# Row-wise log-sum-exp: the last four rows loaded in four unequal parts, their partial sums taken by VectorE

## The chip, the cores and the metric

The kernel runs on one core of one Trainium2 chip. The metric is the device time of one execution in microseconds (us); of several executions the median is given.

The engines that matter here are ScalarE (ACT in the profile: exponentials, logarithms, and a sum along the row if asked for), VectorE (DVE: reductions and elementwise work), TensorE (PE: two tiny matmuls), GpSimd (POOL: a few memsets) and SyncE (SP: it issues the DMA transfers).

## The reference

```python
x = np.random.randn(32, 512, 1024).astype(np.float32)
x_max = np.max(x, axis=-1, keepdims=True)
out = (x_max.squeeze(-1) + np.log(np.sum(np.exp(x - x_max), axis=-1))).astype(np.float32)
```

There are 16384 rows of 1024 float32 values, 64 MiB in all, and one float32 result for each row.

## The kernel before

The 16384 rows are spread over the 128 partitions, so each partition holds NB = 128 rows that lie next to each other in memory. "A row" below means one row in every partition: 128 x 1024 values, 512 KB.

**The fast path and its verdict.** The kernel does not look for a maximum first. It sums the plain exponentials and takes the logarithm. Then it asks whether each sum lies between LOW = 1e-18 and HIGH = 1e18. VectorE compares (`compare`, L281 to L289) with both bounds, two matmuls (L304, L307) count the answers over the partitions, a reduce (L312) makes one whole number of them, and SyncE, VectorE and ScalarE read it and branch (L316 to L321). If the count is not the expected one, a second pass with a maximum follows (L322 to L343); with this input it isn't taken.

**Chunks and the ring.** The rows come in chunks, the table `CHUNKS` at the top. An entry (r, n, p, h) means: r rows in one transfer; ScalarE takes the Exp of the first n rows in p pieces, and VectorE sums them, either by one `reduce_sum` for each piece (L255) or, with h true, "by halves", one instruction for each row that adds the row's two halves and sums the result along the way (L242). The other r - n rows ScalarE sums itself, one instruction for each row with an accumulator (L262). The chunks go through a ring of 51 rows in SBUF. SyncE issues all loads in order on one queue (`load`, L155; the last chunk at L146). Before a load it waits until the engines have finished with the rows that lie in its slots: `busy` holds, for each slot, the count of ScalarE's or VectorE's instructions to wait for. Chunks 0 to 3 fill the ring (4, 15, 16 and 16 rows); chunk 4 reuses the slots of chunks 0 and 1, and so on.

**The end.** The last four chunks have one row each. ScalarE sums them itself, into a tile `late` in PSUM; the very last one stands at L225. `take_logs` (L162) takes the logarithms in three pieces: the first 81 rows ahead of chunk 7, the next 43 rows just ahead of the last Exp, the last four after it. The first two pieces go out in one store of 124 columns (L276), the last four in one of 4 columns (L278). VectorE takes the maximum and the minimum of the 124 early sums (L293, L294), compares these two, and then, when the last Ln is done, the four late sums: K = 6 columns in all. SyncE ends when the verdict has been read and both stores have landed (L346 to L349).

**Order.** The program is written out instruction by instruction, and nothing reorders it. Each engine works through its own queue; waits are explicit counts of the semaphores `act_done`, `dve_done`, `landed` and a few more. The code of the last rows:

```python
take_logs(logged, late_row, sums[:, logged:late_row], *done_before[-LATE])
early_logs = acts
for k, (lo, hi) in enumerate(spans):
    nc.scalar.wait_ge(landed[i + k], 16)
    nc.scalar.activation(
        out=ring[:, s, lo:hi], in_=ring[:, s, lo:hi], func=Exp,
        accum_out=late[:, LATE - 1 + k : LATE + k],
    ).then_inc(act_done, 1)
```

Of the kernel before, what the change touches and what calls it, by code (L numbers as in the profile page):

```python
# [9 lines left out]
CHUNKS = [  # L10
    (4, 4, 1, False), (15, 15, 1, False), (16, 16, 2, False), (16, 16, 2, False),
    (16, 15, 2, False), (14, 14, 2, False), (13, 12, 2, False), (9, 8, 1, False),
    (7, 7, 1, True), (5, 4, 1, True), (4, 3, 1, True), (3, 3, 1, False), (2, 2, 1, True),
    (1, 0, 1, False), (1, 0, 1, False), (1, 0, 1, False), (1, 0, 1, False),
]

CUTS = ()
# [3 lines left out]
UNEVEN = ()  # L21
PARTS = ((0, 128, 2), (1, 128, 4), (3, 128, 8), (7, 64, 8), (71, 128, 8))


LN_AT = 7
LN_LAG = 1


LATE = 4
# [9 lines left out]
def kernel(  # L39
# [15 lines left out]
    assert sum(r for r, *_ in CHUNKS) == NB  # L55
# [10 lines left out]


    assert CHUNKS[-1][0] == 1
    spans = list(zip((0, *CUTS), (*CUTS, D)))
    assert 1 <= len(spans) <= 2  # L70
    n_late = LATE - 1 + len(spans)

    K = 2 + n_late

    ring = nc.alloc_sbuf_tensor("ring", [P, RING_ROWS, D], fp32).ap()
    sums = nc.alloc_sbuf_tensor("sums", [P, NB], fp32).ap()
# [3 lines left out]
    ends = nc.alloc_sbuf_tensor("ends", [P, 2], fp32).ap()  # L80
# [7 lines left out]
    TOO_MANY = 2048.0  # L88
    assert TOO_MANY > ALL_GOOD

    landed = [nc.alloc_semaphore(f"landed{i}") for i in range(len(CHUNKS) + len(spans) - 1)]
# [28 lines left out]
    for r, *_ in CHUNKS:  # L120
        if slot + r > RING_ROWS:
            slot = 0
        place.append((slot, row))
        slot += r
        row += r
# [9 lines left out]
    def load(i):  # L135
        (s, row), r = place[i], CHUNKS[i][0]
        act_wait = max(a for a, _ in busy[s : s + r])
        dve_wait = max(d for _, d in busy[s : s + r])
        if dve_wait:
            nc.sync.wait_ge(dve_done, dve_wait)  # L140
        if act_wait:
            nc.sync.wait_ge(act_done, act_wait)
        dst, src = ring[:, s : s + r], x_v[:, row : row + r]
        if i == len(CHUNKS) - 1:
            for k, (lo, hi) in enumerate(spans):
                nc.sync.dma_start(out=dst[:, :, lo:hi], in_=src[:, :, lo:hi]).then_inc(  # L146
                    landed[i + k], 16
                )
        elif i in UNEVEN:
            for first, last, step in PARTS:  # L150
                nc.sync.dma_start(
                    out=dst[first:last:step], in_=src[first:last:step]
                ).then_inc(landed[i], 16)
        else:
            nc.sync.dma_start(out=dst, in_=src).then_inc(landed[i], 16)  # L155
# [10 lines left out]

    late_row = place[-LATE][1]
    assert not any(n_dve for _, n_dve, _, _ in CHUNKS[-LATE:])

    def total(t):  # L170
        return late[:, t - late_row : t - late_row + 1] if t >= late_row else sums[:, t : t + 1]
# [38 lines left out]

    logged = 0
    done_before = [(0, 0)]
    for i, (r, n_dve, parts, by_halves) in enumerate(CHUNKS):
# [3 lines left out]
        if i == LN_AT:  # L217
            logged = place[i - LN_LAG][1]
            take_logs(0, logged, sums[:, :logged], *done_before[i - LN_LAG])
        if i == len(CHUNKS) - 1:  # L220
            take_logs(logged, late_row, sums[:, logged:late_row], *done_before[-LATE])
            early_logs = acts
            for k, (lo, hi) in enumerate(spans):
                nc.scalar.wait_ge(landed[i + k], 16)
                nc.scalar.activation(  # L225
                    out=ring[:, s, lo:hi],
                    in_=ring[:, s, lo:hi],
                    func=Exp,
                    accum_out=late[:, LATE - 1 + k : LATE + k],
                ).then_inc(act_done, 1)  # L230
                acts += 1
            continue
        nc.scalar.wait_ge(landed[i], 16 * (len(PARTS) if i in UNEVEN else 1))
        for lo, hi in cuts(n_dve, parts):
# [5 lines left out]
            if by_halves:  # L240
                for j in range(lo, hi):
                    nc.vector.tensor_tensor_reduce(  # L242
                        out=ring[:, s + j, : D // 2],
                        in0=ring[:, s + j, : D // 2],
                        in1=ring[:, s + j, D // 2 :],
                        scale=1.0,
                        scalar=0.0,
                        op0=Alu.add,
                        op1=Alu.add,
                        accum_out=sums[:, row + j : row + j + 1],  # L250
                    ).then_inc(dve_done, 1)
                    dves += 1
                    busy[s + j] = (0, dves)
            else:
# [4 lines left out]
                for j in range(lo, hi):  # L259
                    busy[s + j] = (0, dves)  # L260
        for j in range(n_dve, r):
# [8 lines left out]
        done_before.append((dves, acts))  # L270

    take_logs(late_row, NB, late[:, : NB - late_row], dves, acts)


    nc.sync.wait_ge(act_done, early_logs)
    nc.sync.dma_start(out=out_v[:, :late_row], in_=res[:, :late_row]).then_inc(stored, 16)  # L276
    nc.sync.wait_ge(act_done, acts)
    nc.sync.dma_start(out=out_v[:, late_row:], in_=res[:, late_row:]).then_inc(stored, 16)  # L278


    def compare(lo, hi, values):  # L281
        nonlocal dves
        nc.vector.tensor_tensor(  # L283
# [112 lines left out]
```

## Time and profile before

| | |
|---|---|
| time, median of 3 runs | 162.25 us (162.18 to 162.79) |
| the profiled execution's own time | 162.67 us |
| its span, first to last instruction | 161.3 us |
| VectorE busy | 121.9 us, 76% |
| ScalarE busy | 115.1 us, 71% |
| TensorE busy | 0.2 us |
| DMA queue of the loads, packets' share of the span | 97.4% |
| read from HBM | 67.11 MB |

The page's shares of busy time are means over the whole span. In this kernel all engines share one end, so the views to read are the landing times of the loads (the DMA issues give the us from issue to landing), the chain of waits, and the timeline of the last microseconds. The chain of waits puts 49% of the span on transfers into `ring`, 30% on VectorE and 20% on ScalarE.

### The profile page before, as it was taken

How to read it: one execution, taken by the hardware profiler on the slowest of the kernel's cores; microseconds unless marked ns; L12 is line 12 of the kernel's file. 1: busy time of each engine (PE TensorE's matmuls, PEld its weight loads, DVE VectorE, ACT ScalarE, POOL GpSimd, SP SyncE). 2: the span in 40 equal slices, each digit the busy share in tenths (PEclk: the TensorE clock that was granted, in tenths of full speed). 3: DMA queues.
4: the chain of work that ended last, by engine and by line, in shares of the span. 5: the costliest groups of instructions: out<-in, count | busy, mean ns of one | idle time of the engine just before them, and what ended most of it. 6: DMA issues, size and time to landing. Idle time of an engine off the chain costs nothing.

```text
span 161.3 us, 149 instructions
## 1 busy us (share of the span) xinstructions
PE 0.2 (0%) x2; PEld 0.1 (0%) x2; DVE 121.9 (76%) x51; ACT 115.1 (71%) x40; POOL 0.4 (0%) x8
## 2 busy tenths in 40 slices
PE   0000000000000000000000000000000000000000
PEld 0000000000000000000000000000000000000000
DVE  0028000003999999999999699999999999999884
ACT  3170005996079960999419993999199999999996
POOL 1000000000000000000000000000000000000000
DMA  7999799979979989989979999999999999999991
GB/s 256 508 488 442 305 472 520 439 341 520 439 341 520 423 358 520 423 358 520 423 325 455 455 455 439 423 423 423 412 402 430 436 420 410 427 436 412 417 407 42
DMA packets 2737, 67.18 MB, mean 417 GB/s; under 512 B 560, under 2 KB 560, under 8 KB 1072
## 3 DMA queue, kind: packets, MB, share of 16 engines
q1 hardware_dynamic: 2736, 67.18, 97.4%
q14 instruction: 1, 0.01, 0.0%
HBM read 67.11 MB, written 0.07 MB: 416 GB/s over the span
## 4 chain that ended last, share of the span: by engine, by line
DMA 49%; DVE 30%; ACT 20%; issue 0%; PE 0%
DMA ring<-in_x_dram 49%; DVE sums L255 29%; ACT ring L235 17%; ACT ring L262 3%; ACT ring L225 1%; ACT res L162 0%; DVE above L283 0%; PE votes L304 0%; DVE verdict L312 0%; PE votes L307 0%
## 5 line engine op out<-in xcount | busy, mean ns | idle before, releaser
L255 DVE TENSOR_REDUCE sums<-ring 128x8 f32<-128x8192 f32 (+5 forms) x14 | 111.2, 7994 | 37.3 <-ACT ring L235 37.2
L235 ACT ACTIVATE ring<-ring 128x8192 f32<-128x8192 f32 (+6 forms) x18 | 104.4, 5836 | 43.9 <-DMA ring<-in_x_dram 43.9
L242 DVE CUSTOM_DVE_ANT_0 ring<-ring 128x512 f32<-128x512 f32 x16 | 9.9, 684 | 0.0
L262 ACT ACTIVATE ring<-ring 128x1024 f32<-128x1024 f32 x8 | 8.2, 1041 | 0.0
L205 ACT ACT_TABLE_LOAD x1 | 1.3, 1283 | 0.8 <-PEq L377 0.8
L262 ACT ACTIVATION_READ_ACCUMULATOR ring<-ring 128x1 f32 x8 | 1.4, 174 | 0.0
L242 DVE DVE_READ_ACCUMULATOR2_ANT sums<- 128x1 f32 x16 | 1.3, 80 | 0.0
L225 ACT ACTIVATE ring<-ring 128x1024 f32<-128x1024 f32 x1 | 1.0, 1040 | 0.0
L283 DVE TENSOR_TENSOR above<-late,bounds 128x8 bf16<-128x8 f32 x1 | 0.2, 168 | 0.7 <-ACT res L162 0.7
L162 ACT ACTIVATE res<-sums 128x81 f32<-128x81 f32 (+1 forms) x2 | 0.5, 248 | 0.0
L312 DVE TENSOR_REDUCE verdict<-votes 1x1 int32<-1x6 f32 x1 | 0.2, 152 | 0.3 <-PE votes L307 0.3
L293 DVE TENSOR_REDUCE ends<-sums 128x1 f32<-128x124 f32 x1 | 0.3, 282 | 0.1
L304 PE MATMUL votes<-above,weights 128*1 128x6 bf16 x1 | 0.2, 167 | 160.0 <-DVE above L283 160.0
L294 DVE TENSOR_REDUCE ends<-sums 128x1 f32<-128x124 f32 x1 | 0.3, 271 | 0.0
L283 DVE TENSOR_TENSOR above<-ends,bounds 128x4 bf16<-128x4 f32 x1 | 0.2, 162 | 0.1
L162 ACT ACTIVATE res<-late 128x4 f32<-128x4 f32 x1 | 0.2, 173 | 0.0
L304 PEld LDWEIGHTS votes<-above,weights 128*1 128x1 bf16 x1 | 0.1, 80 | 160.0 <-DVE above L283 160.0
L307 PE MATMUL votes<-above,weights 128*1 128x6 bf16 x1 | 0.2, 165 | 0.0
L225 ACT ACTIVATION_READ_ACCUMULATOR ring<-ring 128x1 f32 x1 | 0.2, 153 | 0.0
L206 POOL MEMSET bounds<- 128x6 f32 x1 | 0.1, 104 | 0.4 <-POOLq L377 0.4
L207 POOL MEMSET bounds<- 128x6 f32 x1 | 0.1, 104 | 0.0
L377 POOL MEMSET const-bfloat16-1.0<- 128x1 bf16 x1 | 0.1, 103 | 0.0
(6 smaller groups left out, 0.6 us busy)
## 6 DMA issues: line engine op xcount, KB each, us to landing
ring<-in_x_dram SPq DMA_DIRECT2D x1, 7680.0 KB, 25.1
ring<-in_x_dram SPq DMA_DIRECT2D x1, 7168.0 KB, 28.6
ring<-in_x_dram SPq DMA_DIRECT2D x1, 6656.0 KB, 35.7
ring<-in_x_dram SPq DMA_DIRECT2D x1, 4608.0 KB, 20.3
ring<-in_x_dram SPq DMA_DIRECT2D x2, 2048.0 KB, 16.2
ring<-in_x_dram SPq DMA_DIRECT2D x1, 3584.0 KB, 28.5
ring<-in_x_dram SPq DMA_DIRECT2D x1, 2560.0 KB, 27.5
ring<-in_x_dram SPq DMA_DIRECT2D x4, 512.0 KB, 27.2
```

What stands on the lines that cost most here:

```text
L162: nc.scalar.activation(out=res[:, lo:hi], in_=src, func=Ln, bias=bias).then_inc(act_done, 1)
L205: nc.scalar.preload_act_table_set("natural_log_exp_and_others")
L225: nc.scalar.activation(out=ring[:, s, lo:hi], in_=ring[:, s, lo:hi], func=Exp, accum_out=late[:, LATE - 1 + k : LATE + k],).then_inc(act_d ...
L235: nc.scalar.activation(out=ring[:, s + lo : s + hi], in_=ring[:, s + lo : s + hi], func=Exp).then_inc(act_done, 1)
L242: nc.vector.tensor_tensor_reduce(out=ring[:, s + j, : D // 2], in0=ring[:, s + j, : D // 2], in1=ring[:, s + j, D // 2 :], scale=1.0, scal ...
L255: nc.vector.reduce_sum(out=sums[:, row + lo : row + hi], in_=ring[:, s + lo : s + hi], axis=AX).then_inc(dve_done, 1)
L262: nc.scalar.activation(out=ring[:, s + j], in_=ring[:, s + j], func=Exp, accum_out=total(row + j),).then_inc(act_done, 1)
L283: nc.vector.tensor_tensor(out=above[:, :, lo:hi], in0=values.unsqueeze(1).to_broadcast([P, 2, hi - lo]), in1=bounds[:, :, lo:hi], op=Alu.i ...
L293: nc.vector.reduce_max(out=ends[:, :1], in_=sums[:, :late_row], axis=AX).then_inc(dve_done, 1)
L294: nc.vector.tensor_reduce(out=ends[:, 1:], in_=sums[:, :late_row], axis=AX, op=Alu.min).then_inc(dve_done, 1)
L304: nc.tensor.matmul(votes[:1, :K], lhsT=weights[:, :1], rhs=above[:, 0], start=True, stop=False)
L307: nc.tensor.matmul(votes[:1, :K], lhsT=weights[:, 1:], rhs=above[:, 1], start=False, stop=True).then_inc(counted, 1)
```

## The change

There are two parts. The first is a new table of chunks: how many rows of each chunk VectorE sums, in how many pieces and in which way. The second is the end of the input: the last four rows are no longer four transfers of one row, but one flat stretch of 4096 values in each partition, cut at 1536, 2688 and 3456 into parts of 1.5, 1.125, 0.75 and 0.625 rows. ScalarE takes the Exp of each part as it lands. VectorE sums the first three parts by halves: the piece of each row that a part holds is one instruction, and where a row is continued the instruction starts from the row's sum so far. The last part ScalarE sums itself into `late`, and the last Ln gets VectorE's partial sum of that row as its bias.

With this, the Ln pieces are now the first 67 rows (ahead of chunk 6), the next 60 after the last Exp, and the last row. The first store (67 columns) is issued right after the last loads, the second (61 columns) after the last Ln. The maximum and minimum are taken over the first 94 sums, between the two reduces of chunk 7; the compare takes these two and the other sums one by one, K = 37 columns. The first load, the ring and the second pass are as before.

```diff
 CHUNKS = [
-    (4, 4, 1, False), (15, 15, 1, False), (16, 16, 2, False), (16, 16, 2, False),
-    (16, 15, 2, False), (14, 14, 2, False), (13, 12, 2, False), (9, 8, 1, False),
-    (7, 7, 1, True), (5, 4, 1, True), (4, 3, 1, True), (3, 3, 1, False), (2, 2, 1, True),
-    (1, 0, 1, False), (1, 0, 1, False), (1, 0, 1, False), (1, 0, 1, False),
+    (4, 0, 1, False), (15, 15, 1, False), (16, 16, 1, False), (16, 14, 2, False),
+    (16, 13, 2, False), (14, 12, 2, False), (13, 11, 2, False), (9, 8, 2, False),
+    (7, 6, 1, False), (5, 4, 1, True), (4, 3, 1, True), (3, 3, 1, True), (2, 2, 1, True),
 ]
-CUTS = ()
+LAST_ROWS = 4
+CUTS = (1536, 2688, 3456)
-LN_AT = 7
-LN_LAG = 1
-LATE = 4
+LOG_AT, LOG_UPTO = 6, 4
+EARLY = 6
...
-    K = 2 + n_late
+    K = NB - early_rows + 2 + 1
...
+    def halves(s, row, lo=0, hi=D):
+        nonlocal dves
+        half = (hi - lo) // 2
+        nc.vector.tensor_tensor_reduce(
+            out=ring[:, s, lo : lo + half],
+            in0=ring[:, s, lo : lo + half],
+            in1=ring[:, s, lo + half : hi],
+            scale=1.0,
+            scalar=total(row) if lo else 0.0,
+            op0=Alu.add,
+            op1=Alu.add,
+            accum_out=total(row),
+        ).then_inc(dve_done, 1)
+        dves += 1
+        parts_done[row] = dves
...
+    nc.scalar.wait_ge(pool_done, 1)
...
+                if i == EARLY + 1 and not lo:
+                    nc.vector.wait_ge(dve_done, done_after[EARLY][0])
+                    for k, op in enumerate((Alu.max, Alu.min)):
+                        nc.vector.tensor_reduce(
+                            out=all_sums[:, NB + k : NB + k + 1],
+                            in_=sums[:, :early_rows],
+                            axis=AX,
+                            op=op,
+                        ).then_inc(dve_done, 1)
+                        dves += 1
...
+    s, row = place[-1]
+    wait_free(s, LAST_ROWS)
+    here, there = flat(ring[:, s : s + LAST_ROWS]), flat(x_v[:, row:])
+    for k, (lo, hi) in enumerate(spans):
+        nc.sync.dma_start(out=here[:, lo:hi], in_=there[:, lo:hi]).then_inc(
+            landed[len(CHUNKS) + k], 16
+        )
+
+    nc.sync.wait_ge(act_done, logs_done)
+    nc.sync.dma_start(out=out_v[:, :logged], in_=res[:, :logged]).then_inc(stored, 16)
+    for k, (lo, hi) in enumerate(spans):
+        last = k == len(spans) - 1
+        nc.scalar.wait_ge(landed[len(CHUNKS) + k], 16)
+        nc.scalar.activation(
+            out=here[:, lo:hi],
+            in_=here[:, lo:hi],
+            func=Exp,
+            accum_out=late[:, :1] if last else None,
+        ).then_inc(act_done, 1)
+        acts += 1
+        if not last:
+            rows = list(range(lo // D, -(-hi // D)))
+            if lo % D:
+                rows = rows[1:] + rows[:1]
+                nc.vector.wait_ge(dve_done, parts_done[row + lo // D])
+            nc.vector.wait_ge(act_done, acts)
+            for j in rows:
+                halves(s + j, row + j, max(lo - j * D, 0), min(hi - j * D, D))
+    summed = acts
+    take_logs(logged, NB - 1, sums[:, logged : NB - 1], dves, done_after[-1][1])
+    take_logs(NB - 1, NB, late[:, :1], parts_done[NB - 1], summed, bias=total(NB - 1))
     nc.sync.wait_ge(act_done, acts)
-    nc.sync.dma_start(out=out_v[:, late_row:], in_=res[:, late_row:]).then_inc(stored, 16)
+    nc.sync.dma_start(out=out_v[:, logged:], in_=res[:, logged:]).then_inc(stored, 16)
...
-    nc.vector.wait_ge(act_done, done_before[-LATE][1])
+    nc.vector.wait_ge(act_done, done_after[-1][1])
     nc.vector.wait_ge(dve_done, dves)
-    nc.vector.reduce_max(out=ends[:, :1], in_=sums[:, :late_row], axis=AX).then_inc(dve_done, 1)
-    nc.vector.tensor_reduce(
-        out=ends[:, 1:], in_=sums[:, :late_row], axis=AX, op=Alu.min
-    ).then_inc(dve_done, 1)
-    dves += 2
-    nc.vector.wait_ge(pool_done, 1)
-    nc.vector.wait_ge(dve_done, dves)
-    compare(0, 2, ends)
+    compare(above[:, :, : K - 1], all_sums[:, early_rows:])
     nc.vector.wait_ge(act_done, acts)
-    compare(2, K, late[:, :n_late])
+    compare(above[:, :, K - 1 :], late[:, :1])
```

## The prediction

> **What bounds the kernel now.** I read the page's DMA parts first, then the landing times by issue, then the timeline of the last 12 us.
>
> The page, DMA queues:
>
> ```profile
> q1 hardware_dynamic: 2736, 67.18, 97.4%
> ...
> HBM read 67.11 MB, written 0.07 MB: 416 GB/s over the span
> ```
>
> The timeline of SyncE, and the DMA issues of the same moment (size, us from issue to landing):
>
> ```profile
> 130.07 0.47 SPq L146 DMA_DIRECT2D ring<-in_x_dram  x1
> ```
>
> ```profile
> ring<-in_x_dram SPq DMA_DIRECT2D x1, 512.0 KB, 28.3
> ```
>
> The queue's packets fill 97.4% of the span, and the last load, issued at 130.07, lands 28.3 us later, at 158.4. Read one by one in the same way, the single rows land at 154.6 (128.74 + 25.9), 157.2 (129.59 + 27.6) and 158.4: 1.27 us for each 512 KB. So the loads stream without a hole, and nothing on an engine can move 158.4 unless it lets the queue run dry.
>
> The timeline after that:
>
> ```profile
> 157.35 1.05 ACT L262 ACTIVATE ring<-ring 128x1024 f32<-128x1024 f32 x1
> 157.56 0.69 DVE L242 CUSTOM_DVE_ANT_0 ring<-ring 128x512 f32<-128x512 f32 x1
> 158.17 0.08 DVE L242 DVE_READ_ACCUMULATOR2_ANT sums<- 128x1 f32 x1
> 158.30 0.16 ACT L262 ACTIVATION_READ_ACCUMULATOR ring<-ring 128x1 f32 x1
> 158.35 0.24 ACT L162 ACTIVATE res<-sums 128x43 f32<-128x43 f32 x1
> ...
> 158.49 1.04 ACT L225 ACTIVATE ring<-ring 128x1024 f32<-128x1024 f32 x1
> 158.56 0.27 DVE L294 TENSOR_REDUCE ends<-sums 128x1 f32<-128x124 f32 x1
> 158.61 0.35 SPq L276 DMA_DIRECT2D out_dram<-res  x1
> 158.94 0.16 DVE L283 TENSOR_TENSOR above<-ends,bounds 128x4 bf16<-128x4 f32 x1
> 159.44 0.15 ACT L225 ACTIVATION_READ_ACCUMULATOR ring<-ring 128x1 f32 x1
> 159.62 0.17 ACT L162 ACTIVATE res<-late 128x4 f32<-128x4 f32 x1
> 159.82 0.34 SPq L278 DMA_DIRECT2D out_dram<-res  x1
> ```
>
> The end is a short chain: landing 158.4, Exp of one row 158.49, Ln 159.62 to 159.79, store issued 159.82. The span ends at 161.29. Two things run to that end side by side: the last store (landing 1.4 us after its issue, 161.23), and the verdict (compare, matmuls, reduce, branch), after which SyncE has cleared its semaphores at 161.21 by the trace's sequencer records. Only these 2.9 us behind 158.4 can be shortened.
>
> **The change, part by part.** *The new distribution of rows* (CHUNKS): rows on VectorE's sums go from 119 to 107, rows that ScalarE sums itself, up to chunk 12, from 5 to 17. The groups by form (busy, mean ns of one):
>
> ```profile
> L255 DVE TENSOR_REDUCE sums<-ring 128x6 f32<-128x6144 f32 x2 | 13.0, 6544 | 0.0
> L235 ACT ACTIVATE ring<-ring 128x3072 f32<-128x3072 f32 x2 | 5.5, 2756 | 0.2 <-DMA ring<-in_x_dram 0.2
> L235 ACT ACTIVATE ring<-ring 128x2048 f32<-128x2048 f32 x1 | 1.9, 1892 | 0.0
> ```
>
> The DMA issues, the two stores:
>
> ```profile
> out_dram<-res SPq DMA_DIRECT2D x1, 62.0 KB, 2.2
> ...
> out_dram<-res SPq DMA_DIRECT2D x1, 2.0 KB, 1.4
> ```
>
> A reduce of r rows takes 1.067r + 0.15 us (3.35 for 3, 6.54 for 6, 8.68 for 8), and the next begins 0.08 before its end; a half-sum of a row begins every 0.613 (timeline of 143.9 to 152.5). An Exp of r rows takes 0.853r + 0.19, and the next begins 0.09 before its end; an Exp that sums a row, about 1.05. Chunk 0's four rows, now summed by ScalarE, take it from 7.54 to 11.8; it then idles until 25.88, so they cost 0, as does its new wait for GpSimd's memsets, which end at 1.0.
>
> Does this starve the loads? They wait for slots. Chunk 2 becomes one Exp and one reduce: Exp 45.23 to 59.1, reduce to 76.3; this frees chunk 5's load (72.28 before). Chunk 3's two reduces of 7 end at 83.9 and 91.4; chunk 6's load waits for the second: 91.4 instead of 80.87. Its bytes are wanted when chunk 5's have gone, shortly before 100.85, so 8 us or more are left. Chunks 7 and 8 issue at 105.5 (107.2 before), chunk 9 at 112.7, the last four rows at 128.4 (128.74). So the stream is unchanged: cost 0. If that cover were gone, each us without work would be a us of time. The first store, now 67 columns, is issued at about 130 behind the last loads in the same queue, and cannot delay them.
>
> *The last loads*: 768, 576, 384 and 320 KB at 1.27 us per 512 KB: from chunk 12's landing at 153.35 to 155.26, 156.69, 157.64, 158.43. The same bytes, the same end.
>
> *ScalarE at the end*: chunk 12's Exp starts at 153.57 as now and leaves ScalarE free at 155.36. The parts take 1.47, 1.15, 0.83 and 0.72 (0.853r + 0.19; no form below one row is in the trace: between 0.72 and the 1.04 of a whole row for the last, which would add up to 0.32; I take the straight line, which all forms from 1 to 15 rows follow). They start at 155.36, 156.74, 157.80 and 158.53. The last one's accumulator is read by 159.31, against 159.59 now: **-0.28**. The Ln over the early rows (43 columns, 0.14 from its start to the next, 158.35 to 158.49) has moved from ahead of the last Exp to behind it. It may start 0.05 after the read has started (158.30 to 158.35 now), at 159.21, and the last Ln 0.14 later, 159.35; the read ends at 159.31, so this costs **+0.01**. Its own cover is that read. But it now waits for all of VectorE's half-sums.
>
> *VectorE at the end* is busy without a break from 121.9: chunk 6 to 133.8, chunk 7 with the minimum and maximum moved between its reduces (0.2 each, now beside the loads) to 142.8, chunk 8 one reduce of 6 to 149.3, chunk 9 four half-sums to 151.7, chunk 10 to 153.6. Chunk 11 waits for its Exp: 153.68 to 155.5, chunk 12 to 156.75. The first part's Exp ends at 156.83: row 0 from 156.85 to 157.46, then 256 columns of row 1. For short half-sums the trace has only the 512-column row: 0.613. Bounds: nothing of it scales (0.613 each), or all but the 0.08 of the accumulator read does. I take the second: reduces show 1.04 ns per column, which makes 0.533 of the 0.613. Then 256 columns cost 0.35, 320 0.41, 192 0.28. A wait of VectorE for itself shows at L294 to L283: end 158.83, next start 158.94, so 0.11 after the end. Part two therefore starts not at 157.9 but at 157.97, and ends at 158.73; part three, whose Exp ends at 158.63, starts at 158.77 and hands over its last sum at **159.43** (start of its last piece, 159.06, + 0.28 + 0.09, as 158.26 follows 157.56 now). The 60-column Ln starts at 159.45 instead of 159.21, **+0.24**, and the last Ln at 159.59, against 159.62. A start value or a bias read through a pointer is in no row; I take 0 for each of the three, ends 0 and 0.11, the price of the other small wait just shown; nothing in them can gain.
>
> The Trainium skill, "VectorE: DVE Perf Modes" (The DRAIN you can't avoid), says that a semaphore between chained operations costs nothing extra; the rows above show 0.11 behind an operation's end with a wait, and a start 0.08 before its end without one (L293, 158.36 and 0.28 long, to L294, 158.56). By the rule the end would be about 0.1 earlier; the trace decides.
>
> *The last store* has 61 columns (30.5 KB) instead of 4 (2 KB). Rows: 1.4 us for 2 KB, 2.2 for 62 KB; so +0 to +0.8. Of the 62 KB store's sixteen completions fifteen came 1.40 to 1.55 us after the issue and one at 2.24, while one packet of the instruction queue ran 0.61 us from 159.51; the 2 KB store's came at 1.25 to 1.41. I take halfway between 1.41 and 1.55: **+0.07**. [...]
>
> *The verdict* counts 37 columns instead of 6: the wide compare ends by 159.75, ahead of the last Ln; the two matmuls and the reduce over 31 more columns at 1.04 ns add 0.03 to 0.05, so the verdict ends at 161.23, under the store.
>
> Sum against the profiled execution (span 161.29, its own time 162.67): -0.28 + 0.01 + 0.24 + 0.07 = **+0.04**, so 162.71 there. The median of the runs shown, 162.25, lies 0.42 below that execution; the forecast is 162.25 + 0.04, rounded **162.3**.
>
> **The rivals.** *VectorE is in time.* If the short pieces or the self-wait cost a little less, the 60-column Ln starts at 159.21 and the last Ln at 159.35: -0.27 + 0.07, **162.05**. For it: ScalarE is only 0.2 ahead. Against: VectorE has no pause between 121.9 and 153.6, and enters the parts late.
>
> *VectorE becomes the bound* (the other side). If a short half-sum costs the 0.613 of a full one, part one ends at 158.07, part two at 159.49, and the last sum is handed over at 160.80: the last Ln starts 1.34 later than now, **163.66** with the store. Five short pieces are in the chain; from 0.15 us more for each it decides, since 5 x 0.154 + 0.04 = 0.81. For it: no short form is in the trace. Against: the reduces are straight lines.
>
> *The last store meets a straggler* as the first did at 159.51: -0.03 + 0.83, **163.05**. For it: the store has become more like the first one. Against: one instruction packet in the span, and it may fall elsewhere.
>
> *The stream runs dry* because chunk 6's load is issued 10.5 us later: **163.3** for each us missing beyond the 8. Only a far slower 16-row reduce would do it.
>
> **How the numbers follow.** Forecast 0.62, VectorE in time 0.18, VectorE the bound 0.08, straggler 0.08, dry stream 0.04. 162.3 is the likeliest. The range goes from below the second case, 161.9, to just under the straggler, 163.0; about 2 in 10 is outside. 0.5% is 0.81 us, about what a measurement of this kernel can tell from no change: 161.44 and 163.06. The first two cases and half the straggler are within; slower is most of the bound, half the straggler and the dry stream, 0.11; a gain of 0.81 would have to come from the 2.9 us behind the last landing, 0.03.
>
> **What would show it.** Last load landing at 158.4 to 158.5; last Exp starting near 158.53, 0.72 long; half-sums of 256, 320 and 192 columns starting 0.35, 0.41 and 0.28 apart; the last of them ending near 159.4 and the 60-column Ln waiting for VectorE; the store landing in 1.45 to 1.5. It is wrong if the last landing moves, if a short half-sum takes 0.6, or if the store takes 2.

## The result and the profile after

| | before | after |
|---|---|---|
| time, median of 6 runs each | 162.5 us (162.18 to 162.92) | 163.34 us (163.19 to 163.56) |
| ratio of the times | | 1.0051, 95% interval 1.0032 to 1.0071 |
| the profiled execution's own time / span | 162.67 / 161.29 | 163.19 / 161.81 |
| last load lands (of the 16 DMA engines that carry it, the last one's completion) | 158.42 | 157.95 |
| from there to the end of the span | 2.87 | 3.86 |

The kernel is 0.84 us slower, 0.5%, and the whole interval lies above 1; the forecast of a tie was wrong, and 163.34 lies above the range. Of the 1.05 us between the forecast (162.29 before it was rounded) and 163.34, 0.25 is the level (before measures 162.5 here, 162.25 in the three runs that the forecast started from); 0.80 is the change (0.84 instead of 0.04). The part of the time that lies outside the span is 1.37 us in both kernels, so all of it lies in the span. One profile's landing says little: in e4, e9, e12 and e16 below, which issue the same loads, it lies at 158.41, 158.08, 158.27 and 158.68, and in this profile it came 0.47 earlier than in that of before. What can be compared is the stretch behind it, which is 0.99 longer.

The page's DMA queues of the kernel after (packets, MB, share of 16 engines' span), and two of its DMA issues (KB, us from issue to landing):

```profile
q1 hardware_dynamic: 2736, 67.18, 96.8%
q14 instruction: 2, 0.02, 0.0%
```

```profile
ring<-in_x_dram SPq DMA_DIRECT2D x1, 320.0 KB, 28.4
...
out_dram<-res SPq DMA_DIRECT2D x1, 30.5 KB, 1.5
```

The loads stream as before, and the last store takes what was forecast. The second line is the clue: two packets of the instruction queue where the kernel before has one (both of 8192 bytes; their times, here and below, are those of the trace's DMA records). The timeline of the last microseconds of the kernel after (start, us, engine, line, operation; in brackets idle time ahead of it and who ended it):

```profile
157.61 0.49 DVE L204 CUSTOM_DVE_ANT_0 ring<-ring 128x320 f32<-128x320 f32 x1
...
158.03 0.48 DVE L204 CUSTOM_DVE_ANT_0 ring<-ring,sums 128x256 f32<-128x256 f32 x1
158.44 0.08 DVE L204 DVE_READ_ACCUMULATOR2_ANT sums<- 128x1 f32 x1
158.73 0.15 ACT L294 ACTIVATION_READ_ACCUMULATOR ring<-ring 128x1 f32 x1
158.75 0.36 DVE L204 CUSTOM_DVE_ANT_0 ring<-ring 128x192 f32<-128x192 f32 x1 [0.23 <-DVE sums L204]
...
159.03 0.41 DVE L204 CUSTOM_DVE_ANT_0 ring<-ring,sums 128x192 f32<-128x192 f32 x1
159.37 0.08 DVE L204 DVE_READ_ACCUMULATOR2_ANT sums<- 128x1 f32 x1
159.56 0.24 DVE L221 TENSOR_TENSOR above<-sums,bounds 128x72 bf16<-128x72 f32 x1
159.86 0.25 ACT L150 ACTIVATE res<-sums 128x60 f32<-128x60 f32 x1 [0.98 <-DVE above L221]
160.02 0.24 ACT L150 ACTIVATE res<-late,sums 128x1 f32<-128x1 f32 x1
160.28 0.34 SPq L316 DMA_DIRECT2D out_dram<-res  x1
```

Two holes are to be seen. First, VectorE's piece of 192 columns starts at 158.75, 0.72 behind the start of the piece ahead of it (158.03); a piece of 256 columns with a start value is elsewhere followed after 0.41 (e6, e16). Its Exp had ended by 158.2, and the engine stands idle for 0.23. Second, the 60-column Ln starts at 159.86. VectorE's last sum was handed over at 159.47 by the trace's semaphore records, and VectorE's own wide compare, which waits for the same sum, starts at 159.56. A sequencer is the part of an engine that goes through the program in order, stands at its waits and hands the work on; the waits and branches in the trace are its records. By the records of ScalarE's sequencer the wait had gone through at 159.49, so 0.37 pass between the wait and the Ln; elsewhere such a step takes 0.06 (e5, 159.78 to 159.84). The waits name the compare as the releaser:

```profile
ACT res L150 <- DVE above L221: 1.0, 1, 1.0
```

That is the last event ahead of the Ln, not its cause, as the fourth experiment shows. Each hole is worth 0.31 us (0.72 less 0.41, 0.37 less 0.06).

### The profile page after: what moved, and what is told of

The parts are those of the page before. It is cut to its first block, busy times and chain, and to the rows that moved or that the text cites. A ratio compares the mean times of both kernels' runs of the same rounds, so it can differ in the third digit from the quotient of the medians.

```text
span 161.8 us, 175 instructions
## 1 busy us (share of the span) xinstructions
PE 0.2 (0%) x2; PEld 0.1 (0%) x2; DVE 113.5 (70%) x54; ACT 117.0 (72%) x60; POOL 0.5 (0%) x8
## 3 DMA queue, kind: packets, MB, share of 16 engines
q1 hardware_dynamic: 2736, 67.18, 96.8%
## 4 chain that ended last, share of the span: by engine, by line
DMA 43%; ACT 34%; DVE 22%; issue 1%; SPq 0%; PE 0%; DVEq 0%
DMA ring<-in_x_dram 43%; ACT ring L243 29%; DVE sums L253 20%; ACT ring L271 4%; DVE ring L204 1%; ACT ring L294 1%; DVE above L221 0%; SPq L140 0%; ACT res L150 0%; PE votes L324 0%; DVE verdict L332 0%; DVE sums L204 0%; PE votes L327 0%; DVEq L319 0%; DVEq L307 0%
## 5 line engine op out<-in xcount | busy, mean ns | idle before, releaser
L253 DVE TENSOR_REDUCE sums<-ring 128x6 f32<-128x6144 f32 (+5 forms) x13 | 102.6, 7941 | 46.2 <-ACT ring L243 46.2
L243 ACT ACTIVATE ring<-ring 128x6144 f32<-128x6144 f32 (+7 forms) x17 | 94.0, 5564 | 36.1 <-DMA ring<-in_x_dram 36.1
L271 ACT ACTIVATE ring<-ring 128x1024 f32<-128x1024 f32 x17 | 17.7, 1041 | 5.4 <-DMA ring<-in_x_dram 5.4
L204 DVE CUSTOM_DVE_ANT_0 ring<-ring 128x512 f32<-128x512 f32 (+3 forms) x16 | 9.4, 637 | 0.4 <-DVE sums L204 0.2
L294 ACT ACTIVATE ring<-ring 128x1536 f32<-128x1536 f32 (+3 forms) x4 | 3.9, 1042 | 0.0
L271 ACT ACTIVATION_READ_ACCUMULATOR ring<-ring 128x1 f32 x17 | 3.2, 187 | 0.0
L150 ACT ACTIVATE res<-sums 128x67 f32<-128x67 f32 (+1 forms) x2 | 0.5, 248 | 1.0 <-DVE above L221 1.0
L204 DVE CUSTOM_DVE_ANT_0 ring<-ring,sums 128x256 f32<-128x256 f32 (+1 forms) x2 | 0.9, 448 | 0.0
L294 ACT ACTIVATION_READ_ACCUMULATOR ring<-ring 128x1 f32 x1 | 0.2, 151 | 0.0
```

Source lines behind the costliest of these rows:

```text
L150: nc.scalar.activation(out=res[:, lo:hi], in_=src, func=Ln, bias=bias).then_inc(act_done, 1)
L204: nc.vector.tensor_tensor_reduce(out=ring[:, s, lo : lo + half], in0=ring[:, s, lo : lo + half], in1=ring[:, s, lo + half : hi], scale=1.0 ...
L243: nc.scalar.activation(out=ring[:, s + lo : s + hi], in_=ring[:, s + lo : s + hi], func=Exp).then_inc(act_done, 1)
L253: nc.vector.reduce_sum(out=sums[:, row + lo : row + hi], in_=ring[:, s + lo : s + hi], axis=AX).then_inc(dve_done, 1)
L271: nc.scalar.activation(out=ring[:, s + j], in_=ring[:, s + j], func=Exp, accum_out=total(row + j),).then_inc(act_done, 1)
L294: nc.scalar.activation(out=here[:, lo:hi], in_=here[:, lo:hi], func=Exp, accum_out=late[:, :1] if last else None,).then_inc(act_done, 1)
```

## The experiments

In a recorded text, a letter stands for the theory told beside it; F is the instruction fetch below. The times of all runs first; "span" and "outside" (time less span) are medians over the runs of a kernel, "behind" is the stretch from the last landing to the end in its profiled execution. The runs of before beside them gave 162.44 to 162.6 us, span 161.1 to 161.2, outside 1.36 to 1.38. The median span less "behind" is an estimate of where the last load lands in a median run: 158.3 for the kernel before and 158.1 for the kernel after.

| kernel | us | ratio, interval | span | outside | behind |
|---|---|---|---|---|---|
| e1 new table, old end | 162.92 | 1.0021 [1.0013, 1.0030] | 161.3 | 1.62 | 3.1 |
| e2 old table, new end | 164.29 | 1.0094 [1.0078, 1.0109] | 162.9 | 1.35 | 4.5 |
| e3 no carried sum | 163.16 | 1.0035 [1.0022, 1.0047] | 161.75 | 1.41 | 3.3 |
| e4 compare last | 163.83 | 1.0074 [1.0061, 1.0088] | 162.45 | 1.38 | 4.1 |
| e5 ScalarE shifted | 163.15 | 1.0046 [1.0031, 1.0061] | 161.8 | 1.36 | 3.5 |
| e6 VectorE shifted | 163.52 | 1.0061 [1.0048, 1.0074] | 162.2 | 1.35 | 3.5 |
| e7 both shifted | 163.18 | 1.0043 [1.0031, 1.0055] | 161.85 | 1.34 | 3.2 |
| e8 e7, cut at rows | 163.07 | 1.0037 [1.0024, 1.0050] | 161.7 | 1.37 | 2.9 |
| e9 no fetch in the span | 163.33 | 1.0065 [1.0050, 1.0079] | 161.45 | 1.90 | 3.2 |
| e10 e9, cut at rows | 163.11 | 1.0044 [1.0031, 1.0057] | 161.2 | 1.90 | 2.9 |
| e11 before, longer program | 162.63 | 1.0011 [1.0002, 1.0019] | 161.3 | 1.35 | 2.9 |
| e12 VectorE's fetch hidden | 163.25 | 1.0038 [1.0024, 1.0051] | 161.6 | 1.72 | 3.4 |
| e13 fetch hidden, cut at rows | 163.20 | 1.0043 [1.0029, 1.0057] | 161.8 | 1.37 | 3.5 |
| e14 e1, fetches hidden | 162.70 | 1.0014 [1.0003, 1.0024] | 161.3 | 1.36 | 3.1 |
| e15 both placed, cut at rows | 162.57 | 1.0009 [0.9999, 1.0019] | 161.2 | 1.37 | 3.0 |
| e16 both placed, own cuts | 162.97 | 1.0026 [1.0017, 1.0036] | 161.6 | 1.34 | 3.4 |

**First round: which part of the change, and is it the small waits?** e1 has the new table of rows and keeps the old end; e2 has the new end with the old table.

```diff
 CHUNKS = [
-    (4, 0, 1, False), (15, 15, 1, False), (16, 16, 1, False), ...
+    (4, 4, 1, False), (15, 15, 1, False), (16, 16, 2, False), ...
```

The first edit is e2's, against the kernel after; e1 keeps the upper table, with the four single rows and the code of the kernel before.

> The new distribution of rows with the four single rows of before at the end (their sums by ScalarE, 43-or-more-column Ln ahead of the last Exp, 4-column store). Theory A (the loss is all in the new end, where two Ln wait for VectorE's partial sums): as the kernel before, ratio 0.998 to 1.002, about 162.2 to 162.7 us; the last landing to the last Ln's start is 1.2 us as before. Rival B (the new distribution costs time): 163.2 to 163.5.

> The old distribution of rows up to chunk 12 with the new four parts at the end. Theory A: the loss is here, and larger, since chunk 11 goes back to one reduce of 3.35 us and VectorE enters the parts about 1.4 us later than in the changed kernel: 164.2 to 164.8. Rival B (the distribution costs it): 162.2 to 162.7.

e1 loses 0.37 of the 0.84, but only 0.1 of it in the span (161.3 against 161.2); the rest is outside, 1.62 instead of 1.37. That was a riddle until the third round. e2 is much slower. Its timeline:

```profile
154.23 3.35 DVE L253 TENSOR_REDUCE sums<-ring 128x3 f32<-128x3072 f32 x1 [1.36 <-ACT ring L243]
...
161.42 0.25 ACT L150 ACTIVATE res<-sums 128x60 f32<-128x60 f32 x1 [1.57 <-DVE sums L204]
```

With the old table VectorE still reduces chunk 11 until 157.6 and hands over its last sum at 161.33. So the new end needs the new table; neither is good alone. One more thing is to be seen in e2: its ScalarE program is shorter (45 records instead of 68), and its Ln stands 0.06 behind its wait. The hole is gone there.

e3 lets each carried piece start at zero and writes it to a spare column, so that VectorE waits for itself once less in parts two and three; the earlier part of such a row is left out of the sum. e4 moves the wide compare behind the last Ln, which also puts it on the path of the verdict.

```diff
-            scalar=total(row) if lo else 0.0,
+            scalar=0.0,
...
-            accum_out=total(row),
+            accum_out=spare(row) if lo else total(row),
...
-                nc.vector.wait_ge(dve_done, parts_done[row + lo // D])
```

> The changed kernel in which a continued row's piece goes to a spare column from 0.0, without the pointer to the sum so far and without VectorE's wait for itself; the second pieces of rows 125 and 126 are left out of the results. Theory A with the carry as its price (the 0.11 and 0.22 us waits behind VectorE's own semaphore, and pointer pieces 0.065 longer): the last piece is handed over at 159.0 instead of 159.47, and the time falls by 0.4 to 0.5 us. If the 60-column Ln then starts at once behind the accumulator's read, 0.8. Rival C (the carry costs nothing, only the number of pieces counts): 0.1 at most.

```diff
+    nc.vector.wait_ge(act_done, acts)
     compare(above[:, :, : K - 1], all_sums[:, early_rows:])
-    nc.vector.wait_ge(act_done, acts)
     compare(above[:, :, K - 1 :], late[:, :1])
```

> The changed kernel with VectorE's wide compare behind the last Ln instead of beside the 60-column Ln. In the changed kernel that Ln starts 0.37 us after its semaphore, 0.05 after the compare's end. Rival D (the compare, reading the same sums, holds the Ln up): the Ln starts within 0.1 of its semaphore, at 159.55, and the store 0.3 us earlier, while the verdict gets 0.25 longer; time 0.0 to 0.2 below the changed kernel's. Theory E (the compare has nothing to do with it): the gap stays 0.37 and the time rises by 0.2 to 0.25.

e3 gains about 0.2 of the 0.84, half of what was expected: the carried pieces' 0.065 each and the hole at the third part are gone (VectorE's packet now runs at 157.65, and no hole goes with it), the hole ahead of the Ln stays (0.37). e4 shows that the releaser named by the waits is innocent:

```profile
159.83 0.08 DVE L204 DVE_READ_ACCUMULATOR2_ANT sums<- 128x1 f32 x1
160.31 0.25 ACT L150 ACTIVATE res<-sums 128x60 f32<-128x60 f32 x1 [0.98 <-DVE sums L204]
...
160.85 0.24 DVE L221 TENSOR_TENSOR above<-sums,bounds 128x72 bf16<-128x72 f32 x1 [0.93 <-ACT res L150]
```

VectorE has nothing but its sums ahead of the Ln now, and the Ln still starts 0.48 behind the start of the last read, as in the kernel after (159.37 to 159.86). So the compare is not the cause. The time rose by some 0.4 us, twice what was expected.

**The theory that remained.** In each trace with a hole, an 8 KB packet of the instruction queue follows 1.0 to 1.15 us behind the start of the wait at which the sequencer stood, and that place is the same in the engine's program: ScalarE's at the 62nd to 64th record of the trace, VectorE's at the 51st to 53rd, with a dozen instructions of the second pass ahead of it in its program. So the theory is: at about its 64th instruction a sequencer stops for some 0.3 us, and the next block of the program is fetched. If its engine has work queued, nobody sees it. If the stop falls behind a wait that has just ended, it is paid in full. The engine does not wait for the packet's bytes: the Ln starts at 159.86, the packet at 160.51. What the sequencer does in the 0.3 us, and that the packet brings the next block, no record shows; what can be tested is that the stop belongs to a place of the program. The kernel before has one packet in its span (159.51); by the same count VectorE's stop there lies beside the reduces at L293 and L294, and ScalarE's program with 47 records never gets that far. The Trainium skill, "Runtime: NRT & Kernel Launch" (Instruction fetch mechanics), has the sequencer fetch blocks of 256 instructions in the same way and calls the crossing mostly hidden; here the packets have 8192 bytes, and the crossing is hidden or costs 0.31, by where it falls. The measurement decides.

**Second round: shift the stop.** e5 puts eight one-column Exps at the start of ScalarE's program, e6 eight one-column memsets at the start of VectorE's, e7 both, and e8 cuts the last rows at 1024, 2048, 3072 and 3456 as well, so that no row but the last is carried on.

```diff
-CUTS = (1536, 2688, 3456)
+CUTS = (1024, 2048, 3072, 3456)
...
+    for k in range(8):
+        nc.vector.memset(dummy_v[:, k : k + 1], 0.0)
...
+    for k in range(8):
+        nc.scalar.activation(out=dummy[:, k : k + 1], in_=bounds[:, 0, :1], func=Exp)
```

> The changed kernel with eight tiny Exp (one column each, into a tile nobody reads) at ScalarE's start, where it waits for the first load anyway; nothing else differs, so ScalarE's later instructions stand eight places further on in its program. Theory F (at a fixed place of its program an engine's sequencer stops for 0.3 to 0.4 us to have the next block of instructions fetched; it shows where the instruction there stands right behind a wait that has just ended): the 60-column Ln starts 0.06 us after its semaphore wait instead of 0.37, and the time falls by 0.3. Rival G (the 0.37 belongs to that Ln itself, behind an idle ScalarE): the gap stays 0.37 and the time is unchanged within 0.1.

> The changed kernel with eight one-column memsets at VectorE's start, where it is idle for 38 us, so that VectorE's later instructions stand eight places further on. Theory F: the first piece of part three starts 0.41 us after the piece before it instead of 0.72, and the time falls by 0.3. Rival G (the gap is the price of a continued piece and of the wait for its sum): it stays 0.72, the time is unchanged within 0.1.

> Both shifts together. Theory F: both gaps go, the time falls by 0.5 to 0.65 from the changed kernel's, to a ratio of 1.001 to 1.002 to the kernel before; what is left is VectorE's lateness, as the prediction had it. Rival G: unchanged, ratio 1.005.

> Both shifts, and the last four rows cut at 1024, 2048, 3072 and 3456: three whole rows, then 384 and 640 columns of the last. No row but the last is continued, so there is no carry and no wait of VectorE for itself; ScalarE has one Exp more. Theory F with VectorE's lateness as the rest of the loss: VectorE hands over its last sum before the last accumulator is read, the 60-column Ln starts right behind that read, ratio 0.997 to 1.000. Rival H (the rest of the loss is the store and the verdict of 37 columns, or ScalarE's own lateness): ratio 1.001 to 1.003.

Each hole goes with its own engine's shift and only with it. e5, the last read of VectorE and the Ln behind it:

```profile
159.66 0.08 DVE L205 DVE_READ_ACCUMULATOR2_ANT sums<- 128x1 f32 x1
159.84 0.25 ACT L151 ACTIVATE res<-sums 128x60 f32<-128x60 f32 x1 [0.67 <-DVE sums L205]
```

e6, the second piece of part two, the first of part three, and the Ln:

```profile
159.00 0.48 DVE L205 CUSTOM_DVE_ANT_0 ring<-ring,sums 128x256 f32<-128x256 f32 x1
...
159.41 0.35 DVE L205 CUSTOM_DVE_ANT_0 ring<-ring 128x192 f32<-128x192 f32 x1
...
160.51 0.25 ACT L151 ACTIVATE res<-sums 128x60 f32<-128x60 f32 x1 [0.66 <-DVE above L222]
```

In e5 the Ln follows the read's start by 0.18 instead of 0.48, while the hole at part three stays. In e6 part three follows after 0.41, and the Ln keeps its 0.48. In e7 both are gone, and in e8 the stretch behind the last landing is 2.88, that of before. So both holes belong to places in the programs. The time does not follow: by the ratios e5, e7 and e8 win back only 0.08, 0.13 and 0.23 us, where 0.3 and more was expected, and e6 loses another 0.16. The packets had moved into the stream of loads (ScalarE's to 121.0 to 121.1, VectorE's to 153.9 to 154.1; where no wait held it up, ScalarE's sequencer was far ahead of its engine, which starts its 62nd record only at 150.7 in e5). There a packet takes 0.31 to 0.33 us. Each load is spread over 16 DMA engines, and it has landed when the slowest has. In e7 the sixteen completions of chunk 12, ahead of VectorE's packet, lie within 0.87 us; of those of the first part, behind it, fifteen lie within 0.86 us (154.32 to 155.18), and the last comes 0.71 later, at 155.89. One engine stays behind like this to the end, and the last landing is at 159.07. By the estimate above the last load lands at 158.7 to 158.8 in e6, e7 and e8, some 0.4 later than in the kernel before, but at 158.3 in e5, which has only the early packet among its loads.

**Third round: no fetch in the span, and the fetch alone.** e9 shortens VectorE's program by moving the second pass's code behind it and ScalarE's by giving chunk 0 back to VectorE; e10 is e9 with cuts at rows. e11 is the kernel *before* with forty one-column Exps ahead, which only puts a fetch into its stream.

```diff
-    (4, 0, 1, False), (15, 15, 1, False), ...
+    (4, 4, 1, False), (15, 15, 1, False), ...
...
-    with nc.body("second_vector", valid_engines=vector):
...
+    with nc.body("second_vector", valid_engines=vector):
```

```diff
+    nc.scalar.wait_ge(pool_done, 1)
+    for k in range(40):
+        nc.scalar.activation(out=idle_a[:, k : k + 1], in_=bounds[:, 0, :1], func=Exp)
```

> The changed kernel with both engines' programs shortened instead of lengthened: VectorE's code of the second pass stands behind the first pass and not ahead of it, and chunk 0's four rows are one Exp and one reduce again, seven instructions fewer on ScalarE. No place of the 64th instruction is reached before the verdict, so no block of instructions is fetched in the span. Theory F with its second half (the fetched 8 KB, where it falls among the loads, holds one of the sixteen DMA engines up and delays the last landing; that is why shifting forward did not pay in time): from the last landing to the end 3.2 us instead of 3.86, the last landing as in the changed kernel, ratio 1.000 to 1.002. Rival I (shifting bought nothing in time because something else then ends last): ratio 1.004 to 1.005 as in the changed kernel.

> The same, with the last four rows cut at 1024, 2048, 3072 and 3456, so that no row but the last is continued. Theory F: 2.9 us from the last landing to the end, as in the kernel before and in the shifted kernel with these cuts, and no fetch among the loads: ratio 0.997 to 1.000, the only version here that could beat both. Rival I: 1.003 to 1.004, as with the forward shift.

> The kernel before with forty one-column Exp at ScalarE's start, where it waits for loads until 25.9 us, so that ScalarE's 64th instruction falls at about 130 to 136 us, among the loads and while ScalarE has work queued. Theory F, second half: one 8 KB instruction packet among the loads, no gap on an engine, and the last landing 0.3 to 0.5 us later: ratio 1.002 to 1.003. Rival J (8 KB more on one of sixteen engines is nothing beside 4 MB): ratio 0.999 to 1.001.

The stretch behind the last landing becomes what was expected: 3.23 in e9, 0.63 less than in the kernel after, which is the two holes, and 2.94 in e10. The spans fall, e10's to within 0.1 of that of before, and the time stays, against both theories: the packets run behind the last instruction (e9: 162.04 and 162.37), and the time outside the span grows from 1.37 to 1.90 us. That was e1's riddle too: its packet stands at 163.12. e11 costs 0.18 us (interval 0.03 to 0.31), between what the two theories expected, so it does not decide between them. Its packet ran at 126.5, and behind it, too, one DMA engine lags (the completions of chunk 6 lie within 0.65 us; of chunk 7 fifteen lie within 0.65, and one comes at 1.14), but in its profile the last load lands at 158.40, no later than in that of before.

**Fourth round: hide them.** e12 (chunk 0 back to VectorE, three memsets) puts VectorE's stop behind part two's first piece; e13 shortens ScalarE's program further (chunks 3 and 4 in one Exp) and cuts at rows; e14 is e1 with eight memsets, so that ScalarE's stop falls beside a running Exp and VectorE's at the first compare, which has time to spare.

```diff
-    (4, 0, 1, False), (15, 15, 1, False), ...
+    (4, 4, 1, False), (15, 15, 1, False), ...
...
+    for k in range(3):
+        nc.vector.memset(idle_v[:, k : k + 1], 0.0)
```

```diff
-    (4, 0, 1, False), (15, 15, 1, False), (16, 16, 1, False), (16, 14, 2, False),
-    (16, 13, 2, False), ...
+    (4, 4, 1, False), (15, 15, 1, False), (16, 16, 1, False), (16, 14, 1, False),
+    (16, 13, 1, False), ...
...
-CUTS = (1536, 2688, 3456)
+CUTS = (1024, 2048, 3072, 3456)
```

> The changed kernel with chunk 0's four rows as one Exp and one reduce (ScalarE's program seven instructions shorter, so it has no fetch) and three one-column memsets at VectorE's start: its stop then falls behind the first piece of part two, while that piece runs and after the loads' packets. Theory F with a price for every place: no gap at part three and none at the 60-column Ln, 3.2 us from the last landing to the end, 1.38 to 1.39 outside the span, ratio 1.001 to 1.003. Rival K (the time outside the span grows whenever the gaps go): ratio 1.004 to 1.005 again.

> The same aim with the cuts at 1024, 2048, 3072 and 3456; chunk 3 and 4 have one Exp and one reduce each in place of two, so that VectorE's stop falls behind the compare of the four last columns, where it waits for the verdict's matmuls anyway. Theory F: 2.9 from the last landing to the end, 1.38 outside the span, ratio 0.998 to 1.001. Rival K: 1.003 to 1.004.

> The new distribution with the old end, whose VectorE program was too short to reach its 64th instruction in the span (its profiled execution had 1.56 us outside the span), with eight one-column memsets at VectorE's start, so that the stop falls at the first compare, which has 2 us to spare. Theory F: 1.38 outside the span, ratio 1.000 to 1.001 instead of 1.0021. Rival B (the distribution itself costs 0.3 us): 1.002.

Neither e12 nor e13 reaches the ratio that was expected; both come out near rival K. e12 has no hole at part three or at the Ln, but 0.11 of VectorE's stop shows (the piece of 320 columns is followed after 0.53 instead of 0.42), and a packet runs behind the end (162.38, 1.03 behind ScalarE's branch), outside 1.72. In e13 a packet falls on the last store, at 160.36 for 0.56 us:

```profile
out_dram<-res SPq DMA_DIRECT2D x1, 30.5 KB, 2.1
```

The store takes 2.1 us instead of 1.5 and ends the kernel, while the verdict was through at 161.0. This is the straggler of the prediction, at 0.6 us instead of the 0.8 priced there. So e13's time does not show rival K: outside the span it has 1.37. e14 is the cleanest reading of the table: outside the span 1.36, and **the new distribution of rows alone costs 0.1 us by the medians, 0.23 by the ratio** (interval 0.05 to 0.39), with whatever of the two stops still shows. That lies between the expectation and rival B's 0.3, which the interval does not exclude.

**Fifth round: both where they cost nothing.** Was the loss explained in full? e15 and e16 place each stop behind the landing of one of the last parts, beside work, ahead of the last store: three one-column Exps, three or four memsets, and a wait that is fulfilled already (so that the one behind it becomes an instruction of the sequencer alone); e15 has one more wait on VectorE, and the cuts at rows. The edit of e16:

```diff
+    for k in range(4):
+        nc.vector.memset(idle_v[:, k : k + 1], 0.0)
...
+    for k in range(3):
+        nc.scalar.activation(out=idle_a[:, k : k + 1], in_=bounds[:, 0, :1], func=Exp)
...
+        if k == 2:
+            nc.scalar.wait_ge(act_done, 1)
         nc.scalar.wait_ge(landed[len(CHUNKS) + k], 16)
```

> The changed kernel with cuts at 1024, 2048, 3072 and 3456, and the instruction packets of both engines placed on purpose: three one-column Exps and three one-column memsets ahead of the programs, and two waits split off, so that each sequencer reaches its stop behind the landing of one of the last parts, while its engine still has work. Fetch theory: no idle time in the middle of the end, both packets between 158 and 159.3, so neither among the loads nor on the last store; end 2.9 us behind the last landing, 1.37 us outside the span, span about 161.2, ratio 0.999 to 1.001. If the loss has another part (the table, the parts as such), the span stays above 161.5 and the ratio is 1.002 or more with all of these signs in place.

> The changed kernel with its own cuts, and both instruction packets placed in the same way (three one-column Exps, four memsets, one wait split off ahead of the Exp of the third part). Fetch theory: the first piece of the third part 0.41 us behind the piece before it, the 60-column Ln 0.06 us behind its wait, packets between 158.4 and 159.2, end 3.2 us behind the last landing, 1.37 us outside the span, span about 161.45, ratio 1.001 to 1.002: the predicted tie, less the time that VectorE is late. If the packets are not the cause, the ratio stays at 1.004 or more.

e15, the packets and the end (packets at 158.45 and 159.34):

```profile
q14 instruction: 3, 0.02, 0.0%
```

```profile
158.72 0.36 DVE L206 CUSTOM_DVE_ANT_0 ring<-ring 128x192 f32<-128x192 f32 x1
...
159.01 0.15 ACT L302 ACTIVATION_READ_ACCUMULATOR ring<-ring 128x1 f32 x1
159.19 0.25 ACT L152 ACTIVATE res<-sums 128x60 f32<-128x60 f32 x1
...
159.34 0.24 ACT L152 ACTIVATE res<-late,sums 128x1 f32<-128x1 f32 x1
159.61 0.34 SPq L326 DMA_DIRECT2D out_dram<-res  x1
```

(The third packet is one of 24 bytes at the start.) The Ln starts 0.03 behind the end of ScalarE's own read (159.16); VectorE's last sum, whose wait ends at 159.12, is in time. Span 161.2, outside 1.37, ratio 1.0009: a tie, as expected. So with cuts at rows the new table, the flat stretch in parts and the wider store and compare together cost about 0.1 us (interval 0 to 0.3) once the stops and packets are out of the way. e16, with the change's own cuts:

```profile
158.36 0.49 DVE L206 CUSTOM_DVE_ANT_0 ring<-ring 128x320 f32<-128x320 f32 x1
...
158.90 0.48 DVE L206 CUSTOM_DVE_ANT_0 ring<-ring,sums 128x256 f32<-128x256 f32 x1
...
159.31 0.35 DVE L206 CUSTOM_DVE_ANT_0 ring<-ring 128x192 f32<-128x192 f32 x1
...
160.10 0.25 ACT L152 ACTIVATE res<-sums 128x60 f32<-128x60 f32 x1 [0.47 <-DVE sums L206]
```

No hole at part three or at the Ln, packets at 158.95 and 159.49; 1.0026 where 1.001 to 1.002 was expected. Part of VectorE's stop still shows: the 256-column piece starts 0.53 behind the 320-column one instead of 0.42. Without those 0.11 the Ln would start 1.31 us behind the last landing (158.68), still 0.29 later than the forecast's 1.02. No version here beats the kernel before.

## Why the prediction was wrong

- *The stream is unchanged:* right; 96.8% of the span in packets, the last part 28.4 us from issue to landing, and by the estimate above the last landing is no later than in the kernel before (158.1 and 158.3).
- *ScalarE's parts:* right; the last Exp is 0.72 long, as the straight line had it. It starts 0.15 behind the landing in the kernel after.
- *Short half-sums scale:* right; behind pieces of 256, 320 and 192 columns the next starts after 0.35 (e3), 0.42 and 0.28, so the rival in which VectorE becomes the bound by 0.613 for each is out. The wait for itself costs 0.12, where 0.11 was taken from the rows of before. None of the other rivals took place in the kernel after either.
- *The last store, +0.07:* right, 1.46 us.
- *The failed step: "The 60-column Ln starts at 159.45 instead of 159.21, +0.24".* It started at 159.86, and the last landing came 0.48 earlier than in the forecast, so it is 0.89 late, counted from the landing (1.91 instead of 1.02). That VectorE's last sum came at 159.47, where 159.43 was forecast, is a coincidence of that early landing. The 0.89 are: 0.31, VectorE's sequencer stop ahead of part three; 0.31, ScalarE's ahead of the Ln; and about 0.27 of small terms. Of these, 0.06 is the step from a semaphore to ScalarE's instruction (0.08 without the stop, taken as 0.02), 0.06 the start value read through a pointer (taken as 0; a piece with one takes 0.48 instead of 0.42), 0.10 the first part's Exp, which starts 0.20 behind its landing instead of 0.10, 0.05 and 0.03 the starts of parts two and three; -0.04 and 0.01 make up the rest. The two stops were in no step and no rival: the forecast put 0.02 between the hand-over of VectorE's last sum and the Ln, and 0.39 passed (159.47 to 159.86).
- *The last Ln with its bias from a pointer, taken as 0, ends 0 and 0.11:* it takes 0.24 instead of 0.17 us, +0.07, inside its bounds. With the 0.89, the store's 0.04 and some 0.03 of steps, less the 0.04 that the forecast gains from the landing to the last Ln, it makes up the 0.99.
- *The prediction saw the instruction packet* and used it for the store only: "one instruction packet in the span, and it may fall elsewhere". It did not ask whose packet it was. The count of instructions answers that, by the reading above: ScalarE's program grows from 47 records to 68, past the place where VectorE's already stopped.

The share of each cause in the median is not settled to a tenth: most kernels without a fetch in the holes pay for it in the stream, on the store or outside the span. That e15 ties and e16 loses 0.48 us bounds it: with the stops hidden, the change's own cuts cost some 0.3 to 0.4 us more than cuts at rows (where only the last row is carried on), and the stops about the same again (0.84 less 0.48). The median spans of e9 and e10, with no packet in them, say the same: 0.35 and 0.1 above before, where the kernel after has 0.8 to 0.9. That the time outside the span grows by 0.3 to 0.5 us when a packet runs there was seen in e1, e9, e10 and e12, but nothing here shows what waits for it.

## What to carry to other kernels

Where an end of a few tenths decides, count the instructions of each engine's program, not only their durations: find the packets of the instruction queue in the trace, see at which instruction each engine's sequencer stops, and whether the change moves such a stop behind a wait. Here a stop was best placed beside queued work, behind the last load and ahead of the last store (e15). And compare the stretch from the last landing to the end, not the absolute times of two profiles: the landing itself lay 0.7 us apart here in kernels that issue the same loads. Then check by the runs' times that the stretch's gain has not gone somewhere else, as it did in e7, e9 and e13.

## What the runs showed of the hardware

- At one place of its program, counted here as about the 64th instruction, a sequencer stops for 0.3 us, and 1.0 to 1.15 us behind the wait at which that shows a packet of 8192 bytes runs for 0.31 to 0.70 us. Beside work no cost could be told (e15, a tie), behind a wait a stop costs 0.31. A packet on a last store cost 0.6 (e13, 2.1 instead of 1.5 us).
- A load's landing is that of the slowest of 16 DMA engines: the last load's completions lie 0.5 us apart in the kernel after, 0.7 in that of before, and 1.0 in e16, also without a packet among the loads. Behind a packet one of the sixteen falls back, by 0.71 us in e7 and 0.49 in e11, and stays back. Some 5 us ahead of the last landing that cost about 0.4 us (an estimate, e6 to e8), 30 us ahead of it 0 to 0.3 (e11).
- Time outside the span is not a constant: 1.34 to 1.41 us where the packets lie in the span, 1.6 to 1.9 where one starts 0.7 us or more behind the last instruction (e1, e9, e10, e12). In e13 one starts 0.16 behind it, and outside is 1.37.
